# A hybrid encoder layer on one core: the gate's SiLU moved into the first projection, and linear attention's heads gated and split one by one

## The chip, the cores and the metric

The kernel runs on one core of one Trainium2 chip. The metric is device time in microseconds (us) of one execution. The engines' names: PE is TensorE's matrix multiplications and PEld its weight loads, DVE is VectorE, ACT is ScalarE, POOL is GpSimd and SP is SyncE; the last two issue most of the DMAs here. Each engine works through its own queue of instructions in order, and waits on semaphores where it needs another engine's or a DMA's result.

## The reference

One bidirectional encoder layer over 512 tokens of width 2048. Half of the mixing width is attention (16 heads), half is gated linear attention (GLA, 4 heads with keys of 128 and values of 256). Cut to what matters:

```python
h = rmsnorm(x, attn_norm_w)
proj = h @ w_in
aq, ak, av, gq, gk, gv, gr, glr = jnp.split(proj, split_idx, axis=-1)
attn_out = mixture_of_dilations(aq, ak, av, rel_table)
log_a_f, log_a_b = ...               # from glr
o = gla_causal(q, k, v, log_a_f) + flip(gla_causal(flip(q), flip(k), flip(v), flip(log_a_b)))
o = o * lax.rsqrt(jnp.mean(o * o, axis=-1, keepdims=True) + NORM_EPS)
gla_out = (merge_heads(o) * gla_norm_w) * jax.nn.silu(gr)      # gr: the gate, 512 x 1024
mixed = jnp.concatenate([attn_out, gla_out], axis=-1) @ w_out
x = x + mixed
h = rmsnorm(x, ffn_norm_w)
x = x + (jax.nn.silu(h @ w_gate) * (h @ w_up)) @ w_down
return rmsnorm(x, final_norm_w)
```

## The kernel before

**Products.** Every product is computed in three passes of matmuls with each operand split into a high part and a low rest: high x high, high x low, low x high. ScalarE casts the high part, VectorE subtracts it from the value to get the low part. For weights that come through the plain stream these are L237 (cast) and L218 (low part). The plain stream (`Stream`, `run_job`, L335 to L348) takes a weight matrix in pieces of 512 KB loaded on SP's queue; a piece has two halves, and one half is multiplied into four PSUM banks of 128x512: 12 matmuls, about 2.7 us. The rest (part of w_in, and the FFN) uses a scheme with seven products in place of eight; there L1409 to L1411 build sums of weight blocks on VectorE, L1422 casts high parts on ScalarE and L1427 takes low parts on VectorE, and TensorE's lines are L1504 and L1518.

**Stages** (us of the profiled execution): two jobs for attention's values (6 to 105), the 7-product part of w_in (104 to 339), four jobs for GLA's q, k and v in whose shade attention runs (339 to 613), w_out (613 to 846), the FFN (846 on). w_out has a column block c of 512 per job. The attention half of its rows (k-tiles 0 to 7) can be multiplied before GLA is done: so come first three half-jobs, c = 1, 2, 3 with k 0 to 7 (613 to 729); then a whole job, c = 0 (729 to 773), whose first 8 halves are attention's rows; then three half-jobs c = 1, 2, 3 with k 8 to 15 (773 to 846). Between jobs the evictions (`evac_out`, L1297) add the banks to the residual x, loaded by `load_res` (L1250, four loads on POOL's queue).

**The 7-product part of w_in** has 12 units of 256 columns (times 512 tokens); units 0 to 3 are the gate gr, one per head. A unit's evacuation copies with ScalarE (L1544 to L1552), adds with VectorE (L1538, L1539) and with four accumulating DMAs on POOL's queue (L1563 to L1566). Some steps later `finish` multiplies the tile c_ of 128x1024 by the row factors of the norm (L1661) and stores it to `grd` (the gate) or `qkd` in DRAM (L1662).

**GLA** is a generator for each head, `gla(h)`; its `yield`s cut it into steps. While a job of the plain stream runs, every half gives `rate` credits for steps of the side work; with `fine` they are run after each bank. In order, a head's steps are: log decays (matmul L924, ScalarE L934 to L936, VectorE L937), their difference (L946), scans (L952), centring (L964 to L967), exponentials (L974 to L976), scaled q and k (L983), scores and a transpose on TensorE (L1015, L1018), masking (L1021) and copy (L1025), their sum (L1029), state sums (L1040), decays (ScalarE L1049, VectorE L1059), the output products (L1087), squares (L1095), the root in four small steps (L377 to L386), the scaling on ScalarE (L1103), and four transposes for each of two tiles (L1111) whose eviction (L1114) multiplies by the norm's weight.

**The gate before**: at the start of the third half-job `load_gates` loads all four heads' gates (512 KB each, L876). When the last head is through with its scaling, the generator `gates` is put into `urgent`: it takes ScalarE's table of SiLU, applies SiLU twice a head (L911), multiplies the eight tiles by it on VectorE (L900), and splits each into a high (L896) and low part (L889).

**Credits and work ahead.** `RATES[1]` is 5.0 steps a half in the first three half-jobs; the job c = 0 has rate 1.0 and is not `fine`. `j.ahead` sets how many sums of w_gate's blocks for the FFN (L1478) are made per half of a job; they are stored to DRAM (L1480). `before_out` runs the FFN's first loads, block sums (`ff.sums`, L1409 to L1411 with 256 columns) and splits in the last two half-jobs; its i counts from 0 to 7 in the job c = 2 and from 8 to 15 in the job c = 3.

`tables(name)` loads ScalarE's table of functions (L174) only if the last one asked for was another.

Of the kernel before, what the change touches and what calls it, by code (L numbers as in the profile page):

```python
# [15 lines left out]
F32 = mybir.dt.float32  # L16
F32R = mybir.dt.float32r
U32 = mybir.dt.uint32
AF = mybir.ActivationFunctionType
OP = mybir.AluOpType  # L20
# [3 lines left out]
P = 128  # L24
D = 2048
S = 512
KT = D // P
NH = 16
DH = 64
NG = 4  # L30
# [82 lines left out]
def put(*slots):  # L113
    for s in slots:
        if s.home is not None:
            s.home.free.append(s.i)


def layer(nc, tc, x, attn_norm_w, w_in, rel_table, gw_f, gb_f, gw_b, gb_b, gla_norm_w, w_out,
# [3 lines left out]
    w_gate, w_up, w_down, out = w_gate[0], w_up[0], w_down[0], out[0]  # L123
    pe, act, dve, pool, sp = nc.tensor, nc.scalar, nc.vector, nc.gpsimd, nc.sync
    mm = pe.matmul

    with tc.manual_schedule(), \
# [6 lines left out]
        s4 = Slots(p4, N4, 1024, "b")  # L134
# [27 lines left out]
        wcol = cst.tile([P, 48], F32, name="wcol")  # L162
# [6 lines left out]
        W_ATT, W_FFN, W_GLA, B_F, B_B = 0, 16, 32, 40, 44  # L169

        def tables(name):
            if state["set"] != name:
                state["set"] = name
                act.preload_act_table_set(name)  # L174

        EXP_LN, SILU = "natural_log_exp_and_others", "silu_and_others"
        state = {"credit": 0.0, "set": None, "ahead": 0.0, "big": 0, "gates": 0}


        class Stream:  # L180
# [63 lines left out]
        AHEAD = 3  # L244
# [17 lines left out]
        urgent = deque()  # L262
# [23 lines left out]
        jobs = []  # L286

        class Job:
# [6 lines left out]
            ahead = 0.0  # L295
# [141 lines left out]
        hT = {}  # L437
# [90 lines left out]
        mixf = {}  # L528
        mixh = {}
# [24 lines left out]
        qkd = dr.tile([8, P, 1024], F32, name="qkd")  # L554
# [222 lines left out]
        gout = {}  # L777
# [92 lines left out]

        grd = dr.tile([4, P, 1024], F32, name="grd")

        def load_gates():
            for g in range(4):
                t = s4.get(F32, [P, 2, 512])
                pool.dma_start(out=t.t.rearrange("p b c -> p (b c)"), in_=grd[g])  # L876
                raw_gate.append(t)

        raw_gate = deque()

        def gates():


            yield
            todo, t, n, rounded = deque(), None, 0, None
            while n < 8 or todo or rounded:
                if rounded:
                    (hi, lo), f = rounded
                    dve.tensor_tensor(lo.t, f.t, hi.f, op=OP.subtract)  # L889
                    put(f)  # L890
                    rounded = None
                if todo and not hT:
                    i = todo.popleft()
                    f = mixf.pop(i)
                    mixh[i] = s4.pair()
                    act.copy(mixh[i][0].t, f.t)  # L896
                    rounded = mixh[i], f
                if t:
                    o = gout.pop(n)
                    dve.tensor_tensor(o.t, o.t, t.t[:, 1 - n % 2], op=OP.mult)  # L900
                    mixf[8 + n] = o
                    todo.append(8 + n)
                    n += 1
                    if n % 2 == 0:
                        put(t)
                        t = None
                if not t and raw_gate:
                    t = raw_gate.popleft()
                    tables(SILU)
                    for f in (1, 0):  # L910
                        act.activation(t.t[:, f], t.t[:, f], AF.Silu, scale=1.0 - 2.0 * f)  # L911
                yield

        def gla(h):
# [187 lines left out]
                    c = slice((b % 2) * 256, (b % 2 + 1) * 256)  # L1102
                    act.activation(on.t[:, b], os_[i].t[:, c], AF.Copy, scale=rs[:, b:b + 1])  # L1103
            put(*os_)
            if h == NG - 1:
                urgent.append(gates())
            yield
            for i in range(2):
                tr = ps.get()
                for b in range(4):  # L1110
                    pe.transpose(tr.t[:, b * P:(b + 1) * P],  # L1111
                                 on.t[:, b, i * P:(i + 1) * P], idn)
                o = s2.get()
                dve.tensor_scalar(o.t, tr.t, wcol[:, W_GLA + 2 * h + i:W_GLA + 2 * h + i + 1], None, op0=OP.mult)  # L1114
                put(tr)
                gout[2 * h + i] = o
            yield
            put(on)


        def spin(n):
# [97 lines left out]
                fr.late()  # L1219

        n_front = len(jobs)
        RATES = (2.5, 5.0)
        APART = 12
        for pr in range(2):
            seg = [(w_in, C_GQ + pr * 256), (w_in, C_GK + pr * 256)]
# [15 lines left out]
        def load_res(c):  # L1241
            x1[c] = []
            for _ in range(2):
                o = s4.get(F32, [P, 2, 512])
                for i in range(2):
                    v = Slot()
                    v.t, v.f, v.i, v.home = o.t[:, i], o.t[:, i], o.i, None if i else s4
                    x1[c].append(v)
            for t in range(4):
                pool.dma_start(out=x1[c][t].t, in_=x[t * P:(t + 1) * P, c * 512:(c + 1) * 512])  # L1250
# [73 lines left out]
        def before_out(c):  # L1324
            def f(i):
                run_urgent()
                if c >= 2:
                    i += 8 * (c - 2)
                    if i >= 6:
                        ff.most = 3 if i < 9 else 5  # L1330
                        ff.load()
                    if i in (8, 9, 11, 12, 14):
                        ff.sums(ff.n_sums, halves=True)
                    if i in (13, 15):
                        ff.split((i - 13) // 2)
            return f

        def start_out(c):
            def f():
                if c == 1:  # L1340
                    free_h()
                if c == 3:
                    load_gates()
                load_res(c)
            return f

        def drop_mix(k):
# [2 lines left out]
        def job_out(c, a, z, evac, **kw):  # L1350
            return job("B", [piece512(w_out, c * 512, k) for k in range(a, z, 2)], list(range(a, z)),
                       lambda k: mixh[k], evac, limit=3, **kw)

        for c in (1, 2, 3):
            job_out(c, 0, 8, evac_out(c, True), rate=RATES[1], start=start_out(c))
        n_in = len(jobs)
        for j in jobs[n_front:]:
            j.fine = True
        jobs[n_front + 3].lead = lambda i: AHEAD + (i > 11) + (i > 13)
        j = job_out(0, 0, KT, evac_out(0), rate=1.0, start=start_out(0))  # L1360
        j.drop = lambda k: drop_mix(k) if k < 8 else None
        for j in jobs[n_front + 4:]:
            j.lead = lambda i: AHEAD + 2
# [281 lines left out]
        class Front(Feed):  # L1645
# [13 lines left out]
            def finish(self, u, c_, c):  # L1659
                def do():  # L1660
                    dve.tensor_tensor(c_.t, c_.t, rb[1].t[:, None, :].to_broadcast([P, 2, 512]), op=OP.mult)  # L1661
                    pool.dma_start(out=grd[u] if u < 4 else qkd[u - 4], in_=c)  # L1662
                    put(c_)

                if u == len(self.units) - 1:
                    self.late = do
                else:
                    do()
                yield
# [457 lines left out]
        run_last = finish()  # L2127
        state["sums"] = ff.ahead()
        for n, j in enumerate(jobs):
            j.ahead = 2.0 if n_in <= n < n_out else 1.0 if n_in - 3 <= n < n_in else 0.0  # L2130
        for n, j in enumerate(jobs):
            if n == n_down:
                dn.run()
# [40 lines left out]
```

## Time and profile before

| | us |
|---|---|
| three runs | 2172.18, 2173.84 (median), 2175.34 |
| profiled execution | 2172.39 |
| its span | 2170.6 |
| TensorE busy | 2151.7 |
| VectorE busy | 1824.4 |
| ScalarE busy | 1221.2 |

The span runs from the first to the last instruction of the profiled execution; 1.8 us lie around it. A row of a waits view gives engine, tile and line that waited, the line it waited for, and the total, the number and the longest of the waits. A row of a timeline gives start, duration, engine, line, operation, output and inputs; x2 are two instructions merged, and what stands in brackets is idle time of the engine before it and what ended it. A row by stage gives the bounds, the length, then the busy time of PE, PEld, DVE, ACT and POOL with their counts, the granted clock, the share of DMA and GB/s. A matmul's duration in the trace is longer than its place in the pipeline: back to back they start every 0.23 us (512 columns). Grouped rows give busy time and mean ns of one.

### The profile page before, as it was taken

The numbers are of one execution on the slowest core, as the hardware profiler recorded it, in microseconds if no ns is written. First come the engines' busy times: TensorE is split into PE (matmuls) and PEld (weight loads), VectorE is DVE, ScalarE is ACT, GpSimd is POOL, SyncE is SP. The second block draws the span as 40 slices with busy tenths as digits, with TensorE's granted clock in tenths as the row PEclk, the third lists the DMA queues.
The fourth block names the chain that finished last, engine by engine and source line by source line (L and its number), as shares of the span: only waits on it lengthen the run. The fifth ranks groups of instructions, "written<-read, shape, count | busy, mean of one in ns | idle before, by whom it ended". The sixth has DMA issues, their size and how long they took to land.

```text
span 2170.6 us, 34926 instructions
## 1 busy us (share of the span) xinstructions
PE 2151.7 (99%) x12682; PEld 1898.7 (87%) x12682; DVE 1824.4 (84%) x3161; ACT 1221.2 (56%) x2228; POOL 358.0 (16%) x499
## 2 busy tenths in 40 slices
PE   9999999999999999999999999999999999999998
PEld 7888887888877888888888888888888899999987
DVE  6689996777778769899899898998989888898885
ACT  8455555677655546455555555555555655555562
POOL 0012213111021110021221112211221120021300
PEclk9999999999999999999999999999999999999999
DMA  6467779445365684477766677676776985576982
GB/s 202 138 177 183 178 183 250 151 139 174 123 224 175 235 278 137 136 182 182 187 178 182 181 180 196 173 184 178 177 199 176 267 205 174 180 182 156 289 304 78
DMA packets 264411, 405.71 MB, mean 187 GB/s; under 512 B 19309, under 2 KB 163357, under 8 KB 264238
## 3 DMA queue, kind: packets, MB, share of 16 engines
q1 hardware_dynamic: 205502, 272.49, 39.3%
q0 software_dynamic: 58416, 130.45, 26.4%
q8 instruction: 100, 1.64, 0.3%
q14 instruction: 73, 0.60, 0.1%
q10 hardware_dynamic: 320, 0.53, 0.1%
HBM read 287.47 MB, written 66.39 MB: 163 GB/s over the span
## 4 chain that ended last, share of the span: by engine, by line
PE 58%; DVE 0%; DMA 0%; issue 0%; ACT 0%; DVEq 0%; ACTq 0%
PE ps L1518 24%; PE ps L1504 12%; PE ps L1877 5%; PE ps L1876 5%; PE ps L1875 5%; PE ps L347 1%; PE ps L346 1%; PE ps L348 1%; PE ps L2072 1%; PE ps L2070 1%; PE ps L2071 1%; DMA gd<-b 0%; DVE b L1427 0%; DVE a L2103 0%; DVE a L1538 0%
## 5 line engine op out<-in xcount | busy, mean ns | idle before, releaser
L1422 ACT CAST b<-b 128x768 fp32r<-128x768 f32 (+1 forms) x569 | 518.9, 944 | 370.4 <-DVE b L1427 172.8
L1427 DVE TENSOR_TENSOR b<-b,b 128x768 fp32r<-128x768 f32 (+1 forms) x569 | 597.0, 1084 | 29.8 <-ACT b L1422 18.5
L1518 PE MATMUL ps<-b,b 128*128 128x512 f32 x1656 | 484.1, 393 | 0.4 <-ACT b L1422 0.2
L1518 PE MATMUL ps<-a,b 128*128 128x512 f32 x1368 | 401.0, 394 | 0.2 <-DVE b L1538 0.2
L1518 PEld LDWEIGHTS ps<-b,b 128*128 128x128 f32 x1656 | 280.8, 188 | 31.9 <-ACT b L1422 0.6
L1504 PEld LDWEIGHTS ps<-b,b 128*128 128x128 f32 x1656 | 271.4, 190 | 39.2
L1504 PE MATMUL ps<-b,b 128*128 128x256 f32 x1656 | 296.8, 280 | 0.0
L1504 PEld LDWEIGHTS ps<-a,b 128*128 128x128 f32 x1368 | 227.3, 189 | 36.7 <-DVE b L1427 0.5
L1518 PEld LDWEIGHTS ps<-a,b 128*128 128x128 f32 x1368 | 228.1, 189 | 22.7 <-issue 0.6
L1504 PE MATMUL ps<-a,b 128*128 128x256 f32 x1368 | 245.6, 280 | 0.1
L1409 DVE TENSOR_TENSOR b<-b 128x512 f32<-128x512 f32 x260 | 177.9, 684 | 17.4 <-DMA b<-in_w_down_dram 7.2
L1875 PE MATMUL ps<-b,b 128*128 128x256 f32 x624 | 176.6, 283 | 0.0
L1876 PE MATMUL ps<-b,b 128*128 128x256 f32 x624 | 176.6, 283 | 0.0
L1877 PE MATMUL ps<-b,b 128*128 128x256 f32 x624 | 176.6, 283 | 0.0
L1875 PEld LDWEIGHTS ps<-b,b 128*128 128x128 f32 x624 | 119.8, 192 | 0.0
L1876 PEld LDWEIGHTS ps<-b,b 128*128 128x128 f32 x624 | 119.8, 192 | 0.0
L1877 PEld LDWEIGHTS ps<-b,b 128*128 128x128 f32 x624 | 119.8, 192 | 0.0
L346 PE MATMUL ps<-b,b 128*128 128x512 f32 x296 | 119.0, 402 | 0.0
L1410 DVE TENSOR_TENSOR b<-b,b 128x256 f32<-128x256 f32 x260 | 110.6, 425 | 9.0
L1411 DVE TENSOR_TENSOR b<-b,b 128x256 f32<-128x256 f32 x260 | 110.6, 425 | 8.9
L347 PE MATMUL ps<-b,b 128*128 128x512 f32 x296 | 115.6, 391 | 0.0
L348 PE MATMUL ps<-b,b 128*128 128x512 f32 x296 | 115.6, 391 | 0.0
(301 smaller groups left out, 4190.3 us busy)
## 6 DMA issues: line engine op xcount, KB each, us to landing
b<-in_w_gate_dram SPq DMA_DIRECT2D x109, 512.0 KB, 3.7
b<-in_w_up_dram SPq DMA_DIRECT2D x88, 512.0 KB, 3.8
b<-in_w_down_dram SPq DMA_DIRECT2D x88, 512.0 KB, 5.5
b<-a POOLq DMA_DIRECT2D x162, 256.0 KB, 4.4
b<-in_w_in_dram SPq DMA_DIRECT2D x78, 512.0 KB, 3.8
b<-in_w_out_dram SPq DMA_DIRECT2D x32, 512.0 KB, 6.9
gd<-b POOLq DMA_DIRECT2D x22, 512.0 KB, 4.0
b<-gd SPq DMA_DIRECT2D x22, 512.0 KB, 5.8
```

Of the source, the lines that this page charges most:

```text
L346: mm(o, xh.t[:, c], wh.t[:, w], start=first and not on, stop=False, skip_group_check=on)
L347: mm(o, xh.t[:, c], wl.t[:, w], start=False, stop=False, skip_group_check=on)
L348: mm(o, xl.t[:, c], wh.t[:, w], start=False, stop=last, skip_group_check=on)
L1409: dve.tensor_tensor(s_[:, :, 0:2], r[:, :, 1:3], r[:, :, 0:1].to_broadcast(shape), op=OP.add)
L1410: dve.tensor_tensor(s_[:, :, 2], s_[:, :, 0], r[:, :, 2], op=OP.add)
L1422: act.copy(o, src)
L1427: dve.tensor_tensor(o, src, h, op=OP.subtract)
L1504: mm(o, wl, xh, start=False, stop=end, skip_group_check=True)
L1518: mm(o.rearrange("p (s t) -> p s t", s=2), wh, x_, start=first and p == 0, stop=False, skip_group_check=True)
L1875: mm(o, xh[:, t], wh, start=first and h == 0, stop=False, skip_group_check=True)
L1876: mm(o, xh[:, t], wl, start=False, stop=False, skip_group_check=True)
L1877: mm(o, xl[:, t], wh, start=False, stop=last, skip_group_check=True)
```

## The change

- In the 7-product part of w_in, `finish` applies SiLU to the gate units right after L1661, on ScalarE, and stores each half of the tile by its own DMA. SiLU's table is asked for there, so the tables are loaded in another order.
- `load_gates` and `gates` go. Each head loads its own gate (`load_gate`, one load of 512 KB on POOL's queue) after its scaling has been issued. The eviction of the transposes multiplies by the norm's weight and by the gate in one instruction, and `heads(h)` then splits the head's two tiles in `urgent`.
- Rates: 4.0 in place of 5.0 in the three half-jobs, 4.0 and `fine` in place of 1.0 in the job c = 0.
- The residual loads for c = 1 come at half 3 of their job in place of its start.
- `j.ahead` is 1.25 in place of 1.0 in the first three half-jobs, and 1.0 in place of 2.0 in the half-job c = 2, k 8 to 15.
- `ff.load` starts at i = 3 in place of 6, and `ff.sums` at i = 5, 7, 9, 11, 13 in place of 8, 9, 11, 12, 14.

```diff
+        gate = {}
+        def load_gate(h):
+            gate[h] = s4.get(F32, [P, 2, 512])
+            pool.dma_start(out=gate[h].t.rearrange("p b c -> p (b c)"), in_=grd[h])
+        def heads(h):
+            todo = deque((2 * h, 2 * h + 1))
+            rounded = None
+            while todo or rounded:
+                if rounded:
+                    (hi, lo), f = rounded
                     dve.tensor_tensor(lo.t, f.t, hi.f, op=OP.subtract)
                     put(f)
                     rounded = None
...
+                if todo:
+                    n = todo.popleft()
+                    f = gout.pop(n)
+                    mixh[8 + n] = s4.pair()
+                    act.copy(mixh[8 + n][0].t, f.t)
+                    rounded = mixh[8 + n], f
                 yield
...
             put(*os_)
-            if h == NG - 1:
-                urgent.append(gates())
+            load_gate(h)
             yield
...
-                dve.tensor_scalar(o.t, tr.t, wcol[:, W_GLA + 2 * h + i:W_GLA + 2 * h + i + 1], None, op0=OP.mult)
+                dve.scalar_tensor_tensor(o.t, tr.t, wcol[:, W_GLA + 2 * h + i:W_GLA + 2 * h + i + 1],
+                                         gate[h].t[:, 1 - i], op0=OP.mult, op1=OP.mult)
                 put(tr)
                 gout[2 * h + i] = o
+            put(gate.pop(h))
             yield
             put(on)
+            urgent.append(heads(h))
...
-        RATES = (2.5, 5.0)
+        RATES = (2.5, 4.0)
...
-                    if i >= 6:
+                    if i >= 3:
                         ff.most = 3 if i < 9 else 5
                         ff.load()
-                    if i in (8, 9, 11, 12, 14):
+                    if i in (5, 7, 9, 11, 13):
                         ff.sums(ff.n_sums, halves=True)
...
-                if c == 3:
-                    load_gates()
-                load_res(c)
+                if c != 1:
+                    load_res(c)
...
-            job_out(c, 0, 8, evac_out(c, True), rate=RATES[1], start=start_out(c))
+            job_out(c, 0, 8, evac_out(c, True), rate=RATES[1], start=start_out(c),
+                    before=(lambda i: load_res(1) if i == 3 else None) if c == 1 else None)
         n_in = len(jobs)
+        jobs[n_front + 3].lead = lambda i: AHEAD + (i > 11) + (i > 13)
+        j = job_out(0, 0, KT, evac_out(0), rate=RATES[1], start=start_out(0))
         for j in jobs[n_front:]:
             j.fine = True
-        jobs[n_front + 3].lead = lambda i: AHEAD + (i > 11) + (i > 13)
-        j = job_out(0, 0, KT, evac_out(0), rate=1.0, start=start_out(0))
...
                     dve.tensor_tensor(c_.t, c_.t, rb[1].t[:, None, :].to_broadcast([P, 2, 512]), op=OP.mult)
-                    pool.dma_start(out=grd[u] if u < 4 else qkd[u - 4], in_=c)
+                    if u < 4:
+                        tables(SILU)
+                        for f in (1, 0):
+                            act.activation(c_.t[:, f], c_.t[:, f], AF.Silu, scale=1.0 - 2.0 * f)
+                            pool.dma_start(out=grd[u][:, f * 512:(f + 1) * 512], in_=c_.t[:, f])
+                    else:
+                        pool.dma_start(out=qkd[u - 4], in_=c)
...
-            j.ahead = 2.0 if n_in <= n < n_out else 1.0 if n_in - 3 <= n < n_in else 0.0
+            j.ahead = {n_out: 0.0, n_out - 1: 1.0}.get(n, 2.0 if n_in <= n < n_out else 1.25 if n_in - 3 <= n < n_in else 0.0)
```

More of the change, by code (lines that the diff above doesn't have):

```diff
@@ L176, in layer @@
         EXP_LN, SILU = "natural_log_exp_and_others", "silu_and_others"
-        state = {"credit": 0.0, "set": None, "ahead": 0.0, "big": 0, "gates": 0}
+        state = {"credit": 0.0, "set": None, "ahead": 0.0, "big": 0}
         class Stream:
@@ L891, in gates @@
                     rounded = None
[L892 to L911, printed above, removed]
+                if todo:
[4 more added lines that the diff above has]
+                    rounded = mixh[8 + n], f
                 yield
```

10 lines of the change are left out of this document (removed).

## The prediction

> **What bounds the kernel now.** I read the page first, then the view of TensorE's waits, then busy time by stage.
>
> ```profile
> span 2170.6 us, 34926 instructions
> PE 2151.7 (99%) x12682; PEld 1898.7 (87%) x12682; DVE 1824.4 (84%) x3161; ACT 1221.2 (56%) x2228; POOL 358.0 (16%) x499
> ```
>
> TensorE is busy in all but 18.9 us of the span. The change adds and removes no matmul, so only these 18.9 us can shrink, and any new wait of TensorE adds to them. The profiled execution took 2172.39 us, 1.8 more than its span; the runs' median is 2173.84, 1.45 above it. I sum against 2172.39 and then add 1.45.
>
> ```profile
> PE ps L1087 <- DVE b L1297: 2.3, 1, 2.3
> PE ps L1015 <- DVE a L983: 2.0, 1, 2.0
> PE ps L1087 <- DVE b L1059: 1.7, 2, 1.1
> PE ps L347 <- DVE a L218: 1.7, 2, 1.0
> ```
>
> In all (us, times, longest). The first three, 6.0 us, lie in linear attention; the fourth in a product of w_out. All four name VectorE: these are moments when its queue is late. The stages below (bounds, then busy us of PE, PEld, DVE, ACT, POOL) say where they are: the 7-product part of the first projection, the three first half-jobs of w_out with linear attention's heads, the fourth (16 halves), and the last.
>
> ```profile
> 104.40:339.10 234.70, 234.47 (x1345) 205.57 (x1344) 214.97 (x342) 123.46 (x204) 49.47 (x64) 1.00 0.74 183
> 612.75:647.79 35.04, 32.46 (x156) 26.98 (x155) 27.40 (x56) 21.30 (x51) 11.05 (x21) 1.00 0.86 300
> 647.79:688.87 41.08, 39.99 (x210) 33.90 (x209) 33.35 (x63) 26.10 (x61) 8.62 (x16) 1.00 0.53 183
> 688.87:729.39 40.52, 38.20 (x189) 32.12 (x189) 25.77 (x57) 20.86 (x55) 4.28 (x8) 1.00 0.47 165
> 729.39:772.91 43.52, 43.52 (x194) 36.05 (x193) 34.67 (x71) 16.18 (x32) 4.29 (x8) 1.00 0.87 301
> 819.97:845.77 25.80, 24.13 (x114) 19.57 (x114) 24.07 (x63) 14.53 (x33) 1.40 (x3) 1.00 0.52 178
> ```
>
> TensorE idles 2.58, 1.09 and 2.32 in the three (5.99 together), nothing in the fourth, 1.67 in the last. The granted clock is 1.00 throughout. VectorE has room on average (27.4 of 35.0): the waits come from bursts.
>
> **Linear attention spread out (rate 5 to 4).** Steps of the heads come further apart in the stream of matmuls, so their VectorE work bunches less, and the last head runs on in the fourth half-job, where TensorE never waited and VectorE's own hi/lo work is small. The wait at L1087 for L1297 is of this kind: the eviction of a half-job stood in VectorE's queue ahead of the product that the head needed.
>
> ```profile
> 691.10 1.28 DVE L1297 TENSOR_TENSOR b<-b,ps 128x512 f32<-128x512 f32 x2
> L952 DVE TENSOR_TENSOR_SCAN a<-a,a 128x512 f32<-128x512 f32 x8 | 9.8, 1222 | 0.2
> L983 DVE TENSOR_TENSOR a<-a,a 128x512 f32<-128x512 f32 x16 | 10.2, 683 | 0.0
> L1478 DVE TENSOR_TENSOR b<-b 128x256 f32<-128x256 f32 x84 | 33.9, 418 | 1.8 <-DMA b<-in_w_gate_dram 1.3
> L965 DVE TENSOR_TENSOR small<-small,a 128x3 f32<-128x3 f32 x8 | 1.3, 164 | 0.3
> 722.62 1.57 ACT L1103 ACTIVATE b<-ps,small 128x256 f32<-128x256 f32 x4 [0.58 <-DVE small L386]
> ```
>
> I followed the new order of instructions with these durations (two of 128x512 in a row take 1.28, so each adds 0.6; a half of w_out is 43.52/16 = 2.72 of TensorE, a bank of it 0.68). The product that waited for L983 in head 0 keeps some 0.25 of its 2.0, since at the lower rate it comes later in the stream. The waits at L1087 (2.3 and 1.7) go: in the new order no eviction stands between decay steps and product. But the head's normalization now straddles the eviction. After the end T of the first half-job's matmuls VectorE works on the last eviction until T+0.65 (the rest could go earlier, its banks were complete), then a lo split to 1.25, a scan to 2.4, a half of w_gate and three small ops to 3.2, a difference of 128x512 to 3.8, a lo split to 4.4, two products like L983 to 5.6, four small ops of the normalization to T+6.2. ScalarE then scales for 1.57: T+7.8. TensorE reaches the transposes nine banks after T, at T+6.1, and waits 1.7, say 1.8 with the hand-overs; by the same walk about 0.7 for head 1, nothing for head 2 or, in the fourth half-job, head 3. New waits 0.25+1.8+0.7 = 2.75 against 5.99: **-3.2**. Bounds: all gone, -6.0; the old waits kept beside the new ones, +2.5.
>
> **Gate in the eviction, heads split one by one.** Eight multiplications go; eight evictions of a PSUM tile by a constant take a second tensor.
>
> ```profile
> L900 DVE TENSOR_TENSOR a<-a,b 128x512 f32<-128x512 f32 x8 | 5.5, 684 | 0.0
> L1114 DVE TENSOR_SCALAR a<-ps,wcol 128x512 f32<-128x512 f32 x8 | 5.6, 746 | 6.1 <-PE ps L1111 6.1
> L1746 DVE SCALAR_TENSOR_TENSOR a<-ps,small,a 128x512 f32<-128x512 f32 x31 | 22.1, 746 | 16.0 <-PE ps L2072 13.7 <-PE ps L348 2.3
> ```
>
> The same form exists at L1746 and takes 746 ns as well, so the eviction costs nothing more. VectorE saves 5.5 us, but all near 727 to 745, at the end of the third half-job and in the fourth, where TensorE doesn't wait: 0. The casts and lo splits of the first three heads move from there into the second and third half-jobs; they are in the walk.
>
> The new wait is on VectorE: the eviction needs its head's gate, loaded on POOL's queue only when the scaling has been issued. Behind it in VectorE's queue stand the masks of the next head, w_gate's halves and the lo splits on which w_out's products wait; behind the load on POOL's, the next head's memsets and the q and k loads of the one after.
>
> ```profile
> L876 POOL DMA_DIRECT2D b<-grd x4: 540/543/546, 675.7 to 677.3; - x4
> DMA to landing us min/median/max: 7.3/8.6/10.3
> ```
>
> Those four loads were issued together. One alone should be nearer 7.3. Between issue and use in head 0 lie about 7.9 us by the walk (issue a little ahead of T, use at T+7): it just fits. I take 0; bounds 0 and 10.3-7.9 = 2.4 a head.
>
> **SiLU in the first projection.** After the multiplication of a gate unit ScalarE gets, ahead of its next casts, two SiLUs, and once a table load; POOL two stores of 256 KB in place of one of 512.
>
> ```profile
> 724.21 1.28 ACT L174 ACT_TABLE_LOAD   x1
> 725.51 1.15 ACT L911 ACTIVATE b<-b 128x512 f32<-128x512 f32 x2
> 162.75 0.76 DVE L1538 TENSOR_TENSOR a<-ps,a 128x256 f32<-128x256 f32 x2 [1.17 <-DMA b<-a]
> 164.21 1.22 DVE L1661 TENSOR_TENSOR b<-b,a 128x1024 f32<-128x1024 f32 x1
> 163.62 1.81 ACT L1422 CAST b<-b 128x768 fp32r<-128x768 f32 x2
> 167.76 0.63 PE L1518 MATMUL ps<-b,b 128*128 128x512 f32 x2
> 168.23 1.08 PE L1518 MATMUL ps<-a,b 128*128 128x512 f32 x4
> 149.60 0.69 DVE L1409 TENSOR_TENSOR b<-b 128x512 f32<-128x512 f32 x1 [0.45 <-DMA grd<-b]
> 144.12 1.79 ACT L1422 CAST b<-b 128x768 fp32r<-128x768 f32 x2
> 143.80 1.22 DVE L1661 TENSOR_TENSOR b<-b,a 128x1024 f32<-128x1024 f32 x1
> ```
>
> Unit 1: the casts ran 163.62 to 165.43, their first matmuls at 167.76 and 168.23. Now SiLU waits for L1661's end at 165.43 and runs to 166.6, and the casts, 1.81 for both, end at 168.35. The second is just late: 0.1. Unit 0 has L1661 earlier against its casts (ended 145.02, casts ended 145.91) but pays the table: load to 145.5, SiLU to 146.7, casts to 148.4, 2.5 later than now. Unit 1's had 2.8 of room (168.23-165.43); unit 0's matmuls stand at the same distance: no wait.
>
> Yet the loop closes over VectorE. Its own casts follow ScalarE's, so they start 1.1 later in unit 0 and 0.65 in the others; the accumulating DMAs follow them, and the idle 1.17 at 162.75 shows that the next unit's evacuation waits for just those. Passed on in full, 1.1 comes to unit 1 (wait 1.2) and 0.65 more to each of units 2 and 3: 2.5 in all. L1409 waits for the store's landing, which comes about 1.5 later; behind it stand VectorE's sums and casts of a later step. Bounds 0.1 and 2.5; I take **+0.7**, since the landings of the accumulating DMAs, not their issue, set the pace and can absorb a later issue.
>
> The Trainium skill, "ScalarE: Activation LUTs", section "What ACT_TABLE_LOAD costs", puts a switch of tables at about 2.66 us, a drain of 1.38 included. The row shows 1.28 and the next activation 0.02 after it; by the page unit 0's casts would be late by about 1 us and the sum 1 us higher, and the measurement decides.
>
> The next exponential is now the first of attention, with one more table load ahead of it, for 1.28.
>
> ```profile
> 365.33 0.73 ACT L649 ACTIVATE a<-a,small 128x512 f32<-128x512 f32 x1 [0.83 <-DVE small L641]
> ```
>
> ScalarE stood idle 0.83 before it, and its load needs no operand, so 0.5 is left; the products of that stage wait for L218's casts, which lead. 0, bounds 0 and 1.28. The reload for linear attention and the one that vanishes after w_out meet a TensorE that isn't waiting: 0.
>
> **The FFN's weight sums, two of five moved.** Five groups of sums (2 us of VectorE each, 836.25 to 838.22) were issued at halves 0, 1, 3, 4, 6 of it; now two come in the half-job before, and three at 1, 3, 5.
>
> ```profile
> 796.44:819.97 23.53, 23.53 (x113) 19.73 (x113) 19.13 (x42) 13.09 (x29) 5.06 (x10) 1.00 0.72 242
> 836.25 0.42 DVE L1409 TENSOR_TENSOR a<-b 128x256 f32<-128x256 f32 x1
> 838.22 0.68 DVE L218 TENSOR_TENSOR a<-b,a 128x512 fp32r<-128x512 f32 x1
> 838.96 0.50 PE L347 MATMUL ps<-a,b 128*128 128x512 f32 x1 [0.68 <-DVE a L218]
> 842.24 0.68 DVE L218 TENSOR_TENSOR a<-b,a 128x512 fp32r<-128x512 f32 x1
> 842.97 0.50 PE L347 MATMUL ps<-a,b 128*128 128x512 f32 x1 [0.99 <-DVE a L218]
> ```
>
> Ahead of the first late split stood four groups; now two: it comes 4 us earlier against a lateness of 0.68. Ahead of the second now three: 2 us earlier against 0.68+0.99 in all. The half-job before takes two groups (4 us) and gives up eight of w_gate's sums at L1478 (2 a half to 1), with 23.53-19.13 = 4.4 us of VectorE free. **-1.6**, bounds -1.7 and +1.
>
> x's loads for the second half-job come at half 3, ahead of linear attention's v loads on POOL's queue, the memsets of the masks behind them: 0, upper bound +1. The quarter more of w_gate's sums in each half of the three half-jobs is part of the walk: 0.
>
> **Sum:** -3.2 - 1.6 + 0.7 = -4.1: 2168.3 for an execution like the profiled one, 2169.7 beside the median.
>
> **Rivals.**
> 1. *All the waits go*: -6.0 - 1.7, the first projection at 0.1: -7.6, 2166.2. For it: room of 7 us and more on VectorE in each of the three stages. Against it: the normalization behind the eviction.
> 2. *The waits only change place*: 2.75 becomes 6: then -1.6 + 0.7 = -0.9, 2172.9.
> 3. *The first projection's loop passes delay on in full*: +2.5 in place of 0.7: -2.3, 2171.5; with the exponential's 1.28, 2172.8. For it: the 1.17 idle at 162.75.
> 4. *Late gates (slower)*: the load lands after VectorE has come to the gated eviction. At 10.3, three heads lose 2.4 each, 7.2; the queue behind is late, so linear attention gains nothing: +7.2 - 1.6 + 0.7 = +6.3, 2180.1. It decides from a landing beyond 7.9. For it: a DMA share of 0.86 in the first half-job, and the only landings seen, 7.3 to 10.3. Against it: those were four at once.
>
> **How the numbers follow.** No change means within 0.2%, 4.35 us (2169.5 to 2178.2), about what a measurement of this kernel can tell. Chances: forecast 0.43 (2167 to 2172, a little over half of it faster than the bound, 0.25 and 0.18), rival 1 0.16, rival 2 0.11, rival 3 0.10, rival 4 0.20. Faster 0.41, same 0.39, slower 0.20. The range goes from all waits gone with a run at the fast end (2172.18 is 1.7 under the median), 2164.5, to gates late by half of rival 4's price (3.6 - 0.9 = 2.7) with a run at the slow end (1.5 above the median), 2178.
>
> **What would show it.** Right: idle of TensorE in the three half-jobs near 2.75 and at the transposes (L1111's successor), the waits at L1087 gone; no wait for L218 near 840; six table loads; waits for casts in units 1 to 3 of the gate below 1 us. Wrong: VectorE idle before the gated eviction with the gate's DMA as its releaser (rival 4); waits for L1422's successor of over 2 us (rival 3); or a TensorE that waits where I found slack, above all at products behind the moved loads.

## The result, and the profile after

The changed kernel took 2178.38 us (median of 22 runs, 2175.83 to 2181.30), the kernel before 2174.54 (22 runs, 2172.18 to 2178.55): a ratio of 1.0016, 95% interval 1.0009 to 1.0022. It is slower by 0.16%, where 0.19% faster was forecast; that is within the 0.2% which the prediction calls no change, and just above the upper end of its range, 2178. The profiled execution took 2178.09 us. From its page:

```profile
span 2176.3 us, 34923 instructions
PE 2156.1 (99%) x12682; PEld 1899.3 (87%) x12682; DVE 1821.7 (84%) x3153; ACT 1221.7 (56%) x2229; POOL 359.8 (17%) x503
```

Busy times are nearly the same. The view of TensorE's waits (who waited for whom: total, times, longest) has other lines:

```profile
PE ps L347 <- DVE a L218: 2.0, 1, 2.0
PE ps L1503 <- DVE b L1523: 1.9, 5, 1.0
PE ps L998 <- DVE a L1096: 1.8, 1, 1.8
PE ps L1093 <- ACT b L1086: 1.5, 2, 1.1
PE ps L1503 <- ACT b L1407: 1.1, 5, 0.2
...
PE ps L998 <- DVE a L966: 0.2, 1, 0.2
```

Line numbers have moved: L998 is L1015 of before, L966 is L983, L1093 L1111, L1096 L1114, L1086 L1103, L1503 L1518, L1523 L1538, L1407 L1422, L1412 L1427, L1394 L1409. The waits at the output products (L1087 of before, 4.0 us) are gone. Grown are the waits in the first projection for the evacuation (0.4 before) and for the casts (0.2 before). New are waits for the transposes, and at the next head's scores for the gated eviction L1096; and the two waits for L218 have become one of 2.0. By stage (bounds, length, then the columns as before):

```profile
104.44:343.95 239.51, 236.66 (x1345) 205.31 (x1344) 215.68 (x342) 128.54 (x213) 51.83 (x68) 1.00 0.73 180
617.95:650.31 32.36, 32.19 (x155) 27.05 (x154) 25.19 (x48) 19.06 (x43) 8.04 (x16) 1.00 0.67 239
650.31:685.28 34.97, 33.80 (x163) 27.89 (x162) 30.41 (x63) 21.01 (x52) 10.84 (x21) 1.00 0.63 213
685.28:726.59 41.31, 38.95 (x201) 32.23 (x200) 32.45 (x67) 23.18 (x55) 3.71 (x8) 1.00 0.53 177
726.59:776.71 50.12, 50.12 (x227) 41.81 (x226) 29.46 (x67) 15.40 (x38) 7.13 (x14) 1.00 0.92 314
823.76:850.77 27.01, 25.02 (x114) 20.49 (x113) 25.42 (x58) 16.60 (x39) 3.02 (x6) 0.95 0.39 123
```

| stage | before | after | difference | forecast |
|---|---|---|---|---|
| 7-product part of w_in | 234.54 | 239.51 | +4.97 | +0.7 |
| three half-jobs and c = 0, with the heads | 160.16 | 158.76 | -1.40 | -3.2 |
| last half-job of w_out | 25.80 | 27.01 | +1.21 | -1.6 |
| all the rest | 1750.1 | 1751.0 | +0.9 | 0 |

(Before: the first stage runs from 104.56 to 339.10, the second from 612.75 to 772.91.) The table sets one profiled execution beside another, 5.7 us apart; the medians lie 3.8 apart. The rest's 0.9 us is spread over stages with unchanged work; the mean granted clock was 0.998 in this execution and 0.999 in that of before, and 0.001 of the span is 2.2 us.

### The profile page after: what moved, and what is told of

The parts are those of the page before. It is cut to its first block, busy times and chain, and to the rows that moved or that the text cites. A ratio compares the mean times of both kernels' runs of the same rounds, so it can differ in the third digit from the quotient of the medians.

```text
span 2176.3 us, 34923 instructions
## 1 busy us (share of the span) xinstructions
PE 2156.1 (99%) x12682; PEld 1899.3 (87%) x12682; DVE 1821.7 (84%) x3153; ACT 1221.7 (56%) x2229; POOL 359.8 (17%) x503
## 4 chain that ended last, share of the span: by engine, by line
PE 57%; DVE 0%; DMA 0%; issue 0%; ACT 0%; DVEq 0%; ACTq 0%
PE ps L1503 24%; PE ps L1489 12%; PE ps L1867 5%; PE ps L1868 5%; PE ps L1866 5%; PE ps L348 1%; PE ps L346 1%; PE ps L347 1%; PE ps L2063 1%; PE ps L2061 1%; PE ps L2062 1%; DMA gd<-b 0%; DVE b L1412 0%; DVE a L2094 0%; DVE a L1523 0%
## 5 line engine op out<-in xcount | busy, mean ns | idle before, releaser
L1407 ACT CAST b<-b 128x768 fp32r<-128x768 f32 (+1 forms) x569 | 518.7, 944 | 373.4 <-DVE b L1412 181.7
L1412 DVE TENSOR_TENSOR b<-b,b 128x768 fp32r<-128x768 f32 (+1 forms) x569 | 597.8, 1085 | 36.4 <-ACT b L1407 25.2
L1503 PE MATMUL ps<-b,b 128*128 128x512 f32 x1656 | 484.3, 393 | 0.9 <-ACT b L1407 0.7
L1503 PE MATMUL ps<-a,b 128*128 128x512 f32 x1368 | 401.4, 394 | 2.1 <-DVE b L1523 1.7
L1503 PEld LDWEIGHTS ps<-b,b 128*128 128x128 f32 x1656 | 280.8, 188 | 32.8 <-ACT b L1407 1.5
L1503 PEld LDWEIGHTS ps<-a,b 128*128 128x128 f32 x1368 | 228.0, 189 | 25.6 <-ACT b L1407 2.5
L1394 DVE TENSOR_TENSOR b<-b 128x512 f32<-128x512 f32 x260 | 178.3, 686 | 21.7 <-DMA b<-in_w_down_dram 6.4
```

What stands on the lines that cost most here:

```text
L1394: dve.tensor_tensor(s_[:, :, 0:2], r[:, :, 1:3], r[:, :, 0:1].to_broadcast(shape), op=OP.add)
L1407: act.copy(o, src)
L1412: dve.tensor_tensor(o, src, h, op=OP.subtract)
L1503: mm(o.rearrange("p (s t) -> p s t", s=2), wh, x_, start=first and p == 0, stop=False, skip_group_check=True)
```

## The experiments

Of e3, e4, e5, e6, e7 and e9 there is one execution each, so their stages are read and not their totals.

### The first projection

The theory after the result: VectorE loses time twice in a gate unit, once since its lo parts follow casts that now stand behind SiLU, and once since a block sum (L1394) is given the buffer of c_ and waits for the store's landing. From VectorE's timeline of the changed kernel, units 1 to 3 (start, duration, what it waited for in brackets):

```profile
162.19 0.76 DVE L1523 TENSOR_TENSOR a<-ps,a 128x256 f32<-128x256 f32 x2 [0.19 <-DMA b<-a]
...
166.81 2.18 DVE L1412 TENSOR_TENSOR b<-b,b 128x768 fp32r<-128x768 f32 x2 [0.42 <-ACT b L1407]
...
171.43 0.69 DVE L1394 TENSOR_TENSOR b<-b 128x512 f32<-128x512 f32 x1 [1.84 <-issue]
...
183.61 0.76 DVE L1523 TENSOR_TENSOR a<-ps,a 128x256 f32<-128x256 f32 x2 [0.19 <-DVE a L1524]
...
205.01 0.76 DVE L1523 TENSOR_TENSOR a<-ps,a 128x256 f32<-128x256 f32 x2 [0.19 <-DVE a L1524]
...
214.25 0.69 DVE L1394 TENSOR_TENSOR b<-b 128x512 f32<-128x512 f32 x1 [1.85 <-DMA grd<-b]
...
226.42 0.76 DVE L1523 TENSOR_TENSOR a<-ps,a 128x256 f32<-128x256 f32 x2 [0.19 <-DVE a L1524]
```

and of the kernel before:

```profile
182.12 0.76 DVE L1538 TENSOR_TENSOR a<-ps,a 128x256 f32<-128x256 f32 x2 [0.58 <-DMA b<-a]
...
201.63 0.76 DVE L1538 TENSOR_TENSOR a<-ps,a 128x256 f32<-128x256 f32 x2 [0.82 <-DMA b<-a]
```

Where a row says "issue", the profile names no releaser; in unit 3 the same wait names the store. A unit took 201.63-182.12 = 19.51 before, of which VectorE waited 0.82: 18.7 of work. After the change a unit takes 205.01-183.61 = 21.40, with 0.42, 1.83 and 0.19 of waits: 18.96 of work. So VectorE, which the page shows as 84% busy (in this stage it was 92%, 214.81 of 234.54), has some 0.6 us of room in a unit. What it waits beyond that comes on top of the unit: units 1, 2 and 3 are longer by 2.05, 1.89 and 1.91. Unit 0, which has the table load, is not longer (19.74 after 20.41): its casts cost VectorE 0.68, but it did not wait for the store. TensorE shows only a part of the delay as idle time. In unit 2 its 113 matmuls, busy for 19.51 before, are busy for 20.58 at a granted clock of 1.00, and 0.8 are idle.

Why units 1 to 3 and not unit 0? The second half store of unit 0 landed 3.0 us after its issue, those of units 1 to 3 after 4.9 to 5.0. The one store of before took 4.3, 3.8, 2.9 and 2.9. In unit 1 the second half was issued at 166.40 and VectorE was ready for the buffer at 169.59: with a landing after 3.0 it would have come at 169.4, and the wait of 1.84 would not have been there (an estimate from these rows). So the wait is about what the landing took longer. What made it longer was not tried.

**e1_front_alone.** Only this part of the change, on the kernel of before (its `gates` without SiLU):

```diff
+                    if u < 4:
+                        tables(SILU)
+                        for f in (1, 0):
+                            act.activation(c_.t[:, f], c_.t[:, f], AF.Silu, scale=1.0 - 2.0 * f)
+                            pool.dma_start(out=grd[u][:, f * 512:(f + 1) * 512], in_=c_.t[:, f])
...
-                    tables(SILU)
-                    for f in (1, 0):
-                        act.activation(t.t[:, f], t.t[:, f], AF.Silu, scale=1.0 - 2.0 * f)
```

> The kernel of before with one part of the change alone: SiLU and two half stores per gate unit in the first projection (and so no SiLU when the gates are loaded). Theory: the loss of the change is made in the 7-product part of the first projection, and by nothing else in it: that stage goes from 234.7 to about 239.7 us as in the changed kernel, the rest stays as before, the whole is about 5 us slower than before. Rival: the stage is slower only in company with the moved steps: then it stays within 1 us of 234.7.

2179.67 us against 2174.43, ratio 1.0021 (1.0011 to 1.0030). The stage by its window:

```profile
104.59:343.66 239.07, 236.65 (x1344) 205.35 (x1344) 215.48 (x342) 128.68 (x213) 51.84 (x68) 1.00 0.73 180
```

The stage is 4.5 us longer, so this part alone makes the loss.

**e2_no_silu**: the changed kernel, the gate stored raw at once.

```diff
-                    if u < 4:
-                        tables(SILU)
...
+                    pool.dma_start(out=grd[u] if u < 4 else qkd[u - 4], in_=c)
```

> The changed kernel with the gate stored without SiLU by one DMA of 512 KB, as before (SiLU is left out of the computation altogether). Theory: the stage falls back to about 234.7 us and the whole is about 5 us faster than the changed kernel, some 1 us faster than before (the heads' spreading gains, the last half-job of w_out loses). Rival: with the heads' part a loss too, it is slower than before.

2173.71 against 2174.43, ratio 0.9995 (0.9986 to 1.0005); the stage is back. e2 leaves SiLU out of the computation, as do e3 and e9. The gain of about 1 us over before that was expected is not clear of zero.

```profile
104.82:339.71 234.89, 234.06 (x1346) 205.33 (x1344) 214.91 (x342) 123.42 (x204) 49.76 (x65) 1.00 0.74 184
```

**e3_two_stores** (SiLU out, half stores kept: the two lines `tables(SILU)` and `act.activation` removed) and **e4_one_store**:

```diff
-                            pool.dma_start(out=grd[u][:, f * 512:(f + 1) * 512], in_=c_.t[:, f])
+                        pool.dma_start(out=grd[u], in_=c)
```

> The changed kernel with SiLU left out of the computation, but the two half stores kept. Theory (VectorE waits for the landing of the second half store because it comes late, and ScalarE's casts stand behind SiLU): with both stores issued right after the multiplication the landing is early enough, VectorE's wait at the block sum behind is at most 0.6 us a unit, the stage is at most 1 us over 234.7. Rival (two DMAs in place of one are the cost): the wait stays near 1.8 us a unit and the stage near 238.

> The changed kernel with SiLU kept, but the tile stored by one DMA of 512 KB behind the second SiLU. Theory: the casts are as late as in the changed kernel (0.4 us of VectorE a unit), the one store lands 3 to 4 us after its issue, so VectorE's wait at the block sum falls from 1.8 to about 0.5 us: the stage lies near 236.5. Rival (SiLU ahead of the casts is all the cost): the stage stays at 239.7. Rival (the second DMA is all): 234.7.

e3 gives a stage of 234.73 us (104.82 to 339.55), with one wait at L1394 of 0.58 in unit 0: two stores cost nothing. In units 1 to 3 they landed after 2.4 to 2.9 us. e4 came out against both its theory and its rivals: one store behind SiLU is worse.

```profile
104.90:346.08 241.18, 238.01 (x1344) 205.24 (x1344) 215.48 (x342) 128.67 (x213) 49.19 (x64) 1.00 0.72 178
```

VectorE's timeline of e4, and after it the landing times of its store (L1651):

```profile
184.31 0.75 DVE L1523 TENSOR_TENSOR a<-ps,a 128x256 f32<-128x256 f32 x2 [0.19 <-DVE a L1524]
...
188.93 2.17 DVE L1412 TENSOR_TENSOR b<-b,b 128x768 fp32r<-128x768 f32 x2 [0.42 <-ACT b L1407]
...
194.42 0.69 DVE L1394 TENSOR_TENSOR b<-b 128x512 f32<-128x512 f32 x1 [2.72 <-DMA grd<-b]
...
206.58 0.76 DVE L1523 TENSOR_TENSOR a<-ps,a 128x256 f32<-128x256 f32 x2 [0.19 <-DVE a L1524]
```

```profile
DMA to landing us min/median/max: 3.1/5.6/6.1
```

The unit takes 206.58-184.31 = 22.27: 2.72+0.42+0.19 of waits and again 18.94 of work. The store of 512 KB, issued later, also takes longer to land: 5.3, 5.9 and 6.1 us in units 1 to 3, where the four gate stores of before have 4.3, 3.8, 2.9 and 2.9. So storing in halves had been a gain of 1.7 us in the stage.

**e9_act_only** was to separate the late casts from the late store: raw store at once, six small copies on ScalarE in SiLU's place.

```diff
+                    pool.dma_start(out=grd[u] if u < 4 else qkd[u - 4], in_=c)
+                    if u < 4:
+                        for f in range(6):
+                            act.copy(warm, c_.t[:, f % 2, 0:128])
```

> The changed kernel with the gate stored raw by one DMA right after the multiplication, and in place of SiLU six small ScalarE copies of parts of the tile into an idle one (about 1.2 us of ScalarE at the same place, SiLU left out of the computation). It delays ScalarE's casts as SiLU does, but not the store. Theory (most of the loss is VectorE's wait for the landing of a store that SiLU makes late): the 7-product part takes at most 236.3 us. Rival (the casts behind SiLU are the loss): it takes 238 us or more.

The stage took 237.62 us (106.31 to 343.93), between the two expectations, so it decides for neither; and the stand-in was too long: 1.96 us by ScalarE's timeline where SiLU takes 1.15. VectorE then waits 1.23 for the casts in place of 0.42, none at the store, and a unit takes 205.64-185.11 = 20.53, from its timeline:

```profile
185.11 0.75 DVE L1523 TENSOR_TENSOR a<-ps,a 128x256 f32<-128x256 f32 x2 [0.54 <-PE ps L1503]
...
190.54 2.17 DVE L1412 TENSOR_TENSOR b<-b,b 128x768 fp32r<-128x768 f32 x2 [1.23 <-ACT b L1407]
...
205.64 0.76 DVE L1523 TENSOR_TENSOR a<-ps,a 128x256 f32<-128x256 f32 x2 [0.44 <-DMA b<-a]
```

So a wait for the casts costs as well, as soon as it goes beyond the room; that SiLU's own 0.42 would fit into the 0.6 follows from the accounting, it was not run alone.

### Linear attention

**e7_gate_early**: the load moved ahead of the squares.

```diff
             put(T[0], *qs, *stts)
             if h % 2:
                 put(*gv.pop(h // 2))
+            load_gate(h)
             yield
...
             put(*os_)
-            load_gate(h)
             yield
```

> The changed kernel with a head's gate loaded when its output products have been issued, four steps of the head earlier than now. Theory: VectorE's waits for the gate at the gated eviction (1.4 us in head 0, 4.1 in head 1) go, and with them TensorE's wait of 1.8 us at the next head's scores; the waits for the scaling on ScalarE (1.1 and 0.45) stay; from the first half-job of w_out to the end of the fourth 157 us in place of 158.8. Rival: the place where the stream stands behind VectorE only moves: 158.5 or more.

The changed kernel's VectorE, from its timeline, and the landings of the gate loads (L877):

```profile
660.69 1.41 DVE L1096 SCALAR_TENSOR_TENSOR a<-ps,wcol,b 128x512 f32<-128x512 f32 x2 [1.44 <-DMA b<-grd]
...
692.81 1.41 DVE L1096 SCALAR_TENSOR_TENSOR a<-ps,wcol,b 128x512 f32<-128x512 f32 x2 [4.09 <-DMA b<-grd]
```

```profile
DMA to landing us min/median/max: 6.4/9.2/10.7
```

In e7 no wait for the gate is left (landings 5.5/6.9/7.5), nor TensorE's 1.8 at L998, and the third half-job has 2.04 us less:

```profile
686.01:725.28 39.27, 38.68 (x202) 32.25 (x201) 32.44 (x67) 23.20 (x55) 3.60 (x7) 1.00 0.54 178
```

From 618.68 to 775.40 the four jobs take 156.72, as expected.

### The last half-job of w_out

**e5_sums_back** and **e6_sums_14**:

```diff
-                    if i >= 3:
+                    if i >= 6:
-                    if i in (5, 7, 9, 11, 13):
+                    if i in (8, 9, 11, 12, 14):
-            j.ahead = {n_out: 0.0, n_out - 1: 1.0}.get(n, ...)
+            j.ahead = {n_out: 0.0}.get(n, ...)
```

```diff
-                    if i in (5, 7, 9, 11, 13):
+                    if i in (5, 7, 9, 11, 14):
```

> The changed kernel with the FFN's first loads, its five groups of block sums (halves 8, 9, 11, 12, 14) and the w_gate sums ahead (2 a half) as before. Theory: the last half-job of w_out falls back to the two short waits of before, 0.7 and 1.0 us for L218, in place of one of 2.0, and to 25.9 to 26.0 us in place of 27.2; no dip of the granted clock follows. Rival: the long wait comes from the later end of linear attention, not from the sums: then it stays at 2.0.

> The changed kernel with the fifth group of sums at i = 14 in place of 13, so that it isn't in one half with the first split of the FFN's weights. Theory: between the lo splits of halves 6 and 7 VectorE then has 4 us of work in place of 6; the last lo split comes 2 us earlier, TensorE's wait of 2.0 for it goes to below 0.3, and the last half-job takes 23.7 to 24.2 us. Rival: the last split is held by its cast or its load, not by VectorE's queue: the wait stays over 1 us.

Both as the theory said. e5 has the two waits of before (1.7 together, longest 1.0) and 25.81 us (824.39 to 850.20); e6 has no wait there:

```profile
825.71:849.54 23.83, 23.83 (x113) 19.64 (x112) 22.20 (x53) 15.47 (x35) 2.18 (x4) 1.00 0.41 135
```

What the change had done, on VectorE's timeline:

```profile
824.01 2.47 DVE L1282 TENSOR_TENSOR b<-b,ps 128x512 f32<-128x512 f32 x4
...
830.15 0.69 DVE L218 TENSOR_TENSOR a<-b,a 128x512 fp32r<-128x512 f32 x1 [1.08 <-ACT a L237]
...
840.22 0.68 DVE L218 TENSOR_TENSOR a<-b,a 128x512 fp32r<-128x512 f32 x1
...
842.16 0.42 DVE L1394 TENSOR_TENSOR a<-b 128x256 f32<-128x256 f32 x1
...
844.14 0.95 DVE L1412 TENSOR_TENSOR b<-b,b 128x768 fp32r<-128x768 f32 x1
...
846.21 0.69 DVE L218 TENSOR_TENSOR a<-b,a 128x512 fp32r<-128x512 f32 x1
```

and on that of before:

```profile
818.17 2.52 DVE L1297 TENSOR_TENSOR b<-b,ps 128x512 f32<-128x512 f32 x4
...
826.19 0.69 DVE L218 TENSOR_TENSOR a<-b,a 128x512 fp32r<-128x512 f32 x1 [0.94 <-ACT a L237]
```

Between the last two lo splits stand 6.0 us (840.22 to 846.21) in place of 4.0 before (838.22 to 842.24), where TensorE has a half of 2.72. The time won earlier in the job was not kept. With two groups more in the half-job before, VectorE came to the eviction 0.25 after the stage's start (823.76) and not 1.80 ahead of it (819.97). Both kernels then stood about 1 us for the same cast, with the split behind it at 6.4 and 6.2 after the start. From there on both have two groups up to the last split, which comes at 22.45 in place of 22.27. The split before it comes 1.8 earlier, as TensorE's one wait of 2.0 in place of two shows.

The order alone cost nothing, though. e7 has the same sums and the same wait of 1.99, and its last half-job, read by its window, is as long as that of before:

```profile
822.45:848.26 25.81, 23.82 (x114) 19.64 (x112) 24.21 (x57) 15.44 (x35) 2.18 (x4) 1.00 0.40 126
```

The changed kernel's 27.01 differ from it by the granted clock, 0.95 in place of 1.00. From the end of the wait to the stage's end it took 3.82 us (846.95 to 850.77), e7 2.63 (845.63 to 848.26).

**b15_sums_only**: the kernel of before with this part alone, the last group at 14.

> The kernel of before with the FFN's part of the change alone, mended: loads from half 3, groups of block sums at 5, 7, 9, 11 and 14, w_gate's sums ahead as in the changed kernel. Theory: the last half-job of w_out takes 24.0 us in place of 25.96, the first three half-jobs stay within 0.5 us: about 1.9 us or 0.09% faster than before.

b14_sums_alone, the same with `j.ahead` left at 1.0 in the three half-jobs, gave no result. b15 took 2173.44 against 2174.81, ratio 0.9995 (0.9985 to 1.0004). The last half-job has 23.87 us (822.88 to 846.75), 1.9 less, as expected; but the heads' four jobs took 162.56 (613.27 to 775.83) against 160.16: the longest wait there was 2.7 in place of 2.3, and in the first of them the mean granted clock was 0.95, which is about 1.8 of these 2.4 us. So that half of the expectation missed, and the gain is not clear of zero.

### Versions meant to be faster

**e8_both_mended**: the edits of e7 and e6 together.

> The changed kernel with the early load of the gates and the fifth group at 14, both. Theory: the two gains add (2.0 in linear attention, 3.2 in the last half-job with its dip of the clock), and what is left over the kernel of before is the first projection's 5 us against a gain of 3.4 and 2.0: no change from before within 1.5 us. Rival: they don't add, since the waits move: 2 us or more slower than before.

2173.40 against 2174.79, ratio 0.9996 (0.9987 to 1.0005): the gains add, and all that was won elsewhere pays for the first projection, 239.88 us here.

**h2_sigmoid**: raw gate, SiLU per head without a change of tables, with the edits of e6 and e7.

```diff
+            sg = [s2.get() for _ in range(2)]
+            for f in (1, 0):
+                act.activation(sg[f].t, gate[h].t[:, f], AF.Exp, scale=2.0 * f - 1.0)
+                act.activation(sg[f].t, sg[f].t, AF.Ln, bias=1.0)
+                act.activation(sg[f].t, sg[f].t, AF.Exp, scale=-1.0)
+                dve.scalar_tensor_tensor(gate[h].t[:, f], gate[h].t[:, f], 1.0 - 2.0 * f, sg[f].t, op0=OP.mult, op1=OP.mult)
```

> The changed kernel with the gate stored raw by one DMA as before, and SiLU taken for each head in linear attention as g times exp(-ln(1+exp(-g))), six ScalarE ops and two of VectorE a head without a change of tables; with the early load and the fifth group of sums at 14. Theory: the 7-product part of w_in takes 234.7 us, the last half-job of w_out 24, and the heads pay at most 1 us for 3.3 us more of ScalarE and 1.2 of VectorE a head: in all 5 us faster than before. Rival: the additional work stands ahead of the next head's exponentials and lo parts, and TensorE waits over 1 us more a head: not faster than before by more than 2 us.

The rival held: 2177.93 against 2174.75, ratio 1.0016 (1.0006 to 1.0025). The first projection took 233.97 and the last half-job 23.86, but the heads' four jobs 165.86 (612.23 to 778.09): TensorE waits 4.6 us at the scores for the gated eviction and 3.8 at the transposes for the masking, and in the second and third of these jobs the mean granted clock was 0.96.

**h0_silu_last**: the kernel of before (raw gate, `gates` at the end) with the changed kernel's rates, x loads and sums, the last group at 14, and

```diff
-                if c == 3:
+                if c == 0:
                     load_gates()
-                load_res(c)
+                if c != 1:
+                    load_res(c)
```

> A version meant to beat both: the kernel of before with the changed kernel's rates, x loads and sums ahead, the fifth group of block sums at 14, and the gates loaded at the start of the fourth half-job of w_out (c = 0) and taken through SiLU, multiplied and split only after the last head, as before. No SiLU in the first projection, no load ahead of a gated eviction. Theory: first projection 234.7 us, linear attention with the fourth half-job 157 to 158 (the waits for the scaling of 1.1 and 0.45 us stay), last half-job 24: about 4.5 us faster than before. Rival: the last head now ends inside the fourth half-job, and the eight gated tiles with 9.6 us of VectorE come too late for its rows 8 to 15: TensorE waits 2 us or more there, and the gain is below 2 us.

2168.41 us against 2174.79, ratio 0.9970 (0.9958 to 0.9981): 0.30% faster than before, in six runs, and so below the changed kernel. Its stages, in the same order:

```profile
104.45:339.14 234.69, 234.18 (x1345) 205.39 (x1344) 214.89 (x342) 123.30 (x204) 49.56 (x65) 1.00 0.74 184
613.07:646.11 33.04, 32.67 (x156) 26.90 (x155) 25.50 (x49) 19.15 (x43) 8.40 (x16) 1.00 0.72 250
646.11:680.77 34.66, 33.81 (x163) 27.89 (x162) 29.06 (x60) 19.99 (x50) 9.62 (x19) 1.00 0.58 189
680.77:720.01 39.24, 38.68 (x202) 32.28 (x201) 31.06 (x64) 20.93 (x51) 4.05 (x8) 1.00 0.47 161
720.01:770.15 50.14, 50.14 (x227) 41.80 (x226) 37.14 (x79) 24.41 (x53) 7.89 (x16) 1.00 0.88 311
817.27:841.10 23.83, 23.83 (x113) 19.64 (x112) 22.21 (x53) 15.46 (x35) 2.18 (x4) 1.00 0.42 137
```

The heads take 157.08 in the four jobs, 3.1 less than before, and TensorE idles nowhere in the fourth, though the gating now lies in it: VectorE's 37.1 of 50.1 us there had room for it. By the stages some 5 us are won, 3.1 here and 2.0 in the last half-job; the rest of the 6.4 between the medians isn't located.

## Why the prediction was wrong

1. **First projection: the wrong engine's slack.** The prediction checked SiLU against TensorE's first use of the casts, and that held (no wait of TensorE for the casts shows in units 0 and 1; the five waits for casts are 1.1 in all). It named VectorE's wait for the store's landing ("which comes about 1.5 later; behind it stand VectorE's sums and casts of a later step") and gave it no price. This is the step that failed. The landing came 2.4 to 3.3 later (counted from the multiplication's start in units 1 to 3), and not 1.5: the second half store was issued 1.2 later and took 4.9 to 5.0 us to land. VectorE's wait came to 1.84 in each of these three units, and there was only 0.6 us of room. So the bounds, 0.1 to 2.5, were too narrow; 4.97 was measured. Rival 3 had the right place and the wrong mechanism: the accumulating DMAs did absorb the later issue (VectorE waited 0.19 for them or none).
2. **Last half-job: order, not amount.** "2 us earlier" for the last split counted the groups ahead of it in the job, one of which lay ahead of a cast that VectorE waited for in both kernels. Behind that cast two groups were left, as before, and the fifth group stood with a split in one half. Forecast -1.6; the order by itself made no difference (e7's 25.81 against 25.80), and with that group one half later it is -1.97 (e6). The +1.21 of the profiled execution is the half clock after the wait, which the prediction did not have and which not every execution shows.
3. **Heads: mechanism right, size off.** Idle of TensorE in the four jobs fell from 5.99 to 3.70 (0.17+1.17+2.36). The waits at the output products went, as said; those at the transposes came and were smaller, 1.06 and 0.45 for 1.8 and 0.7; at head 0's scores 0.2 of 2.0 stayed (0.25 was forecast). The missing term is rival 4's: the gate landed late, 9.2 us in the median where the walk left 7.9. VectorE idled 1.4 and 4.1 for it in heads 0 and 1, and that cost TensorE 1.8 (e7), not 7.2, since a late VectorE reaches TensorE only where that needs it next. The stage won 1.40 and not 2.29: TensorE's busy time in it is 0.9 longer, which stays open.
4. **Right:** the gated eviction costs no more (two took 1.41 by the row at 660.69), six table loads (five at L174 and one at L649), the sixth ahead of attention's first exponential, with no wait of TensorE behind it. That load did not use ScalarE's idle 0.83, as the prediction had it: it began at 370.17, after the idle time, and took its 1.28 in full. The row at SiLU's own load agrees with the prediction's row and not with the drain that the Trainium skill, "ScalarE: Activation LUTs", section "What ACT_TABLE_LOAD costs", adds: from ScalarE's timeline of the changed kernel,

```profile
144.13 1.28 ACT L174 ACT_TABLE_LOAD   x1
145.42 1.16 ACT L1650 ACTIVATE b<-b 128x512 f32<-128x512 f32 x2
```

## What to carry to other kernels

Before work is put ahead of an engine's queue, add up the period of every engine in that stage, waits included: an engine 84% busy over the whole had 0.6 us of room in 19.5 here, and the waits beyond that made the unit longer by as much. A store is not done when it is issued: whoever gets its buffer next waits for the landing, so ask who that is, and don't count on the shortest landing seen. Time won in one half of a pipelined job is lost again if a later step waits for a cast in any case; count the work behind that wait, and spread it so that no half holds two of the large pieces. Before a change of one us in a stage is explained, look at the granted clock there.

## What the runs showed of the hardware

After its wait of 1.99 us for L218 the changed kernel's TensorE ran at half speed for some 3 us, though it then had work without a gap. Windows of 2 us:

```profile
846.00:848.00 2.00, 1.05 (x5) 0.87 (x6) 2.00 (x4) 0.00 (x0) 0.00 (x0) 1.00 0.01 3
848.00:850.00 2.00, 2.00 (x7) 1.57 (x6) 2.00 (x4) 0.40 (x1) 0.14 (x1) 0.55 0.91 259
850.00:852.00 2.00, 2.00 (x11) 1.81 (x10) 1.76 (x4) 1.83 (x7) 1.50 (x4) 0.59 0.45 165
```

The granted clock of 0.55 and 0.59 costs about 2 x 0.45 + 2 x 0.41 = 1.7 us. Of this 1.2 lie in the last half-job of w_out, which ends at 850.77; they are the difference between this stage (27.01) and e7's (25.81). It does not follow from the length of the wait alone. e2, e3 and e9 show such a stretch after waits of 2.3, 2.3 and 1.9 in the same place, but e7 and e4 had waits of 1.99 and 1.97 there and a clock of 1.00 after them, and before's wait of 2.3 at L1087 was followed by none. What decides it is open.

The Trainium skill, "TensorE: Matmul & The Clock Gate", section "Part 1: The HAM clock gate (the "warmup" mystery)", has the clock halve after an idle window of about 3.4 us and calls the window free-running, so that the effect varies from run to run. The half rate and the variation agree with these rows; the length does not, since a wait of 1.99 us was enough here.
